# Hyena convolutions on one Trainium2 core: the spectra's complex product for both signs in single VectorE instructions

## The chip, the cores and the metric

The kernel runs on one core of one Trainium2 chip. The metric is the device time of one execution in microseconds. In three runs the kernel before took 1834.95, 1834.99 and 1835.55 us: the median is 1834.99 us.

## What is computed

Two layers of a trunk over 512 latent and 256 context tokens with 1024 features. In each layer a projection feeds three groups of heads: a bidirectional Hyena operator (256 channels), neighbourhood attention and latent attention. Their outputs are joined and projected, and a squared-ReLU MLP follows. The context is computed in layer 0 alone. The part that the change touches is the long convolution inside Hyena, twice per sequence (once per gate):

```python
def _bidir_fftconv(u, h, bias):
    L, C = u.shape[1], u.shape[2]
    k = jnp.concatenate([h[:, 0], jnp.zeros((1, C), h.dtype), h[:0:-1, 1]], axis=0)
    uf = u.astype(F32)
    y = jnp.fft.irfft(jnp.fft.rfft(uf, n=2 * L, axis=1) * jnp.fft.rfft(k, axis=0), n=2 * L, axis=1)[:, :L]
    return (y + uf * bias.astype(F32)).astype(u.dtype)

def _hyena(p, conv_w, conv_b, filt, bias):
    p = _short_conv(p, conv_w, conv_b)
    v, x1, x2 = jnp.split(p, 3, axis=-1)
    z = v
    for o, gate in enumerate((x1, x2)):
        z = gate * _bidir_fftconv(z, filt[:, o], bias[o])
    return z
```

## The kernel before

All matrix products run on TensorE in single precision; large ones are split into three products of rounded halves. VectorE, ScalarE and GpSimd do the elementwise work between, SyncE issues the loads. The program is written as Python generators, one per task; `weave` takes steps from several in turn at given rates, and a scheduler then fixes the order of the instructions on each engine before the program runs. Each engine works through its own list in that order, and waits on semaphores where a value comes from another engine.

The convolution is `hyena(l, s, y, p)`, for layer `l` and stream `s` (0: 512 latent tokens, tiles named with x; 1: 256 context tokens, tiles named with c). It is woven into the neighbourhood attention: the context's in layer 0 with the making of queries and keys (`na_qk`), the latent one of layer 0 with the attention itself (`na_attend`, lines 526 to 579), that of layer 1 with the end of `na_qk` and with `na_attend`. For each of the two orders `o` it does the following.

- The sequence is split into even and odd positions, and both are transformed by matmuls with cosine and sine tables (line 735), for one tile `ft` of 128 frequencies at a time: `ee` from the even half, `oo` from the odd half, each 128x512 in PSUM (real part and imaginary part, 256 channels each). The latent stream has n = 2 such tiles, the context n = 1.
- ScalarE copies `ee` to SBUF (`eb`, line 739). The sum `eb + oo` is the spectrum at one set of frequencies (sign 0), the difference that at the mirrored set (sign 1), line 744.
- Each is multiplied by the filter's spectrum `kk[:, ft, sgn]`, which is loaded from DRAM. A complex product takes two multiplies (lines 748 and 749, the second with real and imaginary part of the filter exchanged), a subtraction (750) and an addition (751). For sign 1 these four run on GpSimd, for sign 0 on VectorE.
- Sum and difference of the two products go to `z` (lines 753 and 754), from which TensorE transforms back: in the first order with line 763, multiplied by the gate in line 765, in the second with line 774, multiplied by the gate in line 778.

PSUM has four banks `b` here, used in turn by the transforms, by the attention's transposes (560), and by its value products (579). A bank goes to a new user when the last reader of the old one is done; the reader of `oo` is line 744. The attention's scores (526) have two larger buffers `mm`, read by the bias sum on VectorE (548) and its counterpart on ScalarE (549). The softmax then runs through VectorE's maximum (425), ScalarE's exponential (430), VectorE's reciprocal (433), and the normalization of one head on VectorE (438) and of the other on ScalarE (436).

The lines of the product before:

```python
for sgn, op in ((1, ALU.subtract), (0, ALU.add)):
    eng = pool if sgn else dve
    us = p([128, 2, 256], tag=f"us{sgn}{g}")
    dve.tensor_tensor(us, eb..., oo..., op)
    ks = kk[:, ft, sgn]
    ta = p([128, 2, 256], tag=f"ta{sgn}{g}")
    eng.tensor_tensor(ta, us, ks, ALU.mult)
    eng.tensor_tensor(us, us, ks[:, ::-1, :], ALU.mult)
```

Of the kernel before, what the change touches and what calls it, by code (L numbers as in the profile page):

```python
# [16 lines left out]
ALU = mybir.AluOpType  # L17
# [24 lines left out]
def kernel(ctx, tc, A, dbg=None, stop=None):  # L42
    nc = tc.nc
    pe, act, dve, pool, sp = nc.tensor, nc.scalar, nc.vector, nc.gpsimd, nc.sync
# [54 lines left out]
    def b_tile():  # L99
        npsum[0] += 1  # L100
        return ps.pool.tile([128, 512], F32, tag="b", name=f"b{npsum[0]}", bufs=ps.b)
# [199 lines left out]
    def load(p, name, shape, src=None, tag=None, bufs=1):  # L301
        t = p(shape, tag=tag, bufs=bufs)
        sp.dma_start(t, A[name] if src is None else src)
        return t
# [400 lines left out]
    def hyena(l, s, y, p):  # L705
        L, t0 = ((S, 0), (LC, S))[s]
        n = L // 256
        nt = 2 * n
        kd = (kx[l], kc)[s]
        g = "xc"[s]  # L710
        fc = load(p, "dft_f" + g, [128, n, 4, L // 2])
        ic = load(p, "dft_i" + g, [128, n, 4, L // 2])

        def tparity(tile_, m, tt):
            par, i = divmod(tt, n)
            v = tile_[:, m, t0:t0 + L].rearrange("p (t z) -> p t z", z=2)
            return v[:, i * 128:(i + 1) * 128, par]

        u, x1 = p([128, nt, 256], tag="u" + g, bufs=1), p([128, nt, 256], tag="x1" + g)
        for tt in range(nt):  # L720
            t = b_tile()
            for m in range(4):
                pe.transpose(t[:, m * 128:(m + 1) * 128], tparity(y, m, tt), ident)
            act.activation(u[:, tt], t[:, 0:256], AF.Copy)
            act.activation(x1[:, tt], t[:, 256:512], AF.Copy)
            yield
        for o in range(2):
            kk = load(p, None, [128, n, 2, 2, 256], kd[:, :, :, o], "kk" + g)
            z = p([128, n, 2, 2, 256], tag="z" + g)
            for ft in range(n):  # L730
                ee, oo = b_tile(), b_tile()
                for par, out in ((0, ee), (1, oo)):
                    for q in range(2):
                        for kt in range(n):
                            pe.matmul(out[:, q * 256:(q + 1) * 256],  # L735
                                      fc[:, kt, 2 * par + q, ft * 128:(ft + 1) * 128], u[:, par * n + kt],
                                      start=(kt == 0), stop=(kt == n - 1))
                eb = p([128, 512], tag="eb" + g)
                act.activation(eb, ee, AF.Copy)
                y2 = []  # L740
                for sgn, op in ((1, ALU.subtract), (0, ALU.add)):
                    eng = pool if sgn else dve
                    us = p([128, 2, 256], tag=f"us{sgn}{g}")
                    dve.tensor_tensor(us, eb.rearrange("p (i c) -> p i c", i=2),
                                      oo.rearrange("p (i c) -> p i c", i=2), op)
                    ks = kk[:, ft, sgn]
                    ta = p([128, 2, 256], tag=f"ta{sgn}{g}")
                    eng.tensor_tensor(ta, us, ks, ALU.mult)  # L748
                    eng.tensor_tensor(us, us, ks[:, ::-1, :], ALU.mult)
                    eng.tensor_sub(ta[:, 0], ta[:, 0], ta[:, 1])  # L750
                    eng.tensor_add(ta[:, 1], us[:, 0], us[:, 1])
                    y2.append(ta)
                dve.tensor_add(z[:, ft, 0], y2[1], y2[0])
                dve.tensor_sub(z[:, ft, 1], y2[1], y2[0])
                yield
            if o == 0:
                u = p([128, nt, 256], tag="u" + g, bufs=1)
                for tt in range(nt):
                    par, i = divmod(tt, n)
                    t = b_tile()  # L760
                    for ft in range(n):
                        for q in range(2):
                            pe.matmul(t[:, 0:256], ic[:, ft, 2 * par + q, i * 128:(i + 1) * 128], z[:, ft, par, q],  # L763
                                      start=(ft == 0 and q == 0), stop=(ft == n - 1 and q == 1))
                    dve.tensor_mul(u[:, tt], t[:, 0:256], x1[:, tt])
                    yield
            else:
                for ct in range(2):
                    t = b_tile()
                    h = L // 2  # L770
                    for par in range(2):
                        for ft in range(n):
                            for q in range(2):
                                pe.matmul(t[:, par * h:(par + 1) * h], z[:, ft, par, q, ct * 128:(ct + 1) * 128],  # L774
                                          ic[:, ft, 2 * par + q, :], start=(ft == 0 and q == 0),
                                          stop=(ft == n - 1 and q == 1))
                    ys = y[:, 4 + ct, t0:t0 + L].rearrange("p (t z) -> p z t", z=2)
                    dve.tensor_mul(ys, ys, t[:, :L].rearrange("p (z t) -> p z t", z=2))
                    yield
# [422 lines left out]
    for l in range(DEPTH):  # L1202
# [49 lines left out]
        if last:  # L1252
            hs = Pool(f"hy{l}", "right")
            conv = hyena(l, 0, y, hs)
        sc = Pool(f"nas{l}")
        nb = na_bias(l, bp, sc)
        if last:
            weave((na_qk(l, hh, hl, na, sc), 1.0), fill=(conv, H1))
        else:
            weave((na_qk(l, hh, hl, na, sc), 1.0), (hyena(l, 1, y, sc), 0.8))  # L1260
# [17 lines left out]
        if not last:  # L1278
            hs = Pool(f"hy{l}")
            conv = hyena(l, 0, y, hs)  # L1280
# [50 lines left out]
        for m in range(KD):  # L1331
            ks = range(8)
            if last:
                ks = range(4, 8)
# [14 lines left out]
            for s, a, b in STREAM[:len(streams)]:  # L1349
                g = gains[:, l, 1, m, s:s + 1]  # L1350
# [187 lines left out]
```

## Time and profile before

| | |
|---|---|
| median of three runs | 1834.99 us |
| profiled execution, its own time | 1833.48 us |
| span of that execution, first to last instruction | 1831.7 us |
| TensorE busy | 1752.5 us (96%) |
| VectorE busy | 1233.4 us (67%), 2247 instructions |
| ScalarE busy | 754.7 us (41%) |
| GpSimd busy | 135.8 us (7%), 177 instructions |
| mean granted TensorE clock | 0.981 of 2.4 GHz |

The profile is one execution. Its times are microseconds from the span's start; in its rows PE is TensorE, DVE VectorE, ACT ScalarE, POOL GpSimd, SP SyncE, and L748 is line 748 of the kernel. A matmul's record shows its tile, `out<-in`; single-precision matmuls of 128 rows are two records each. The context's convolution lies between 233 and 276 us, layer 0's latent one between 299 and 357 us, that of layer 1 between 1265 and 1323 us. An instruction of VectorE ends some 0.08 us after the next one has begun when neither waits for the other, so a busy time is a little longer than the distance from start to start.

### The profile page before, as it was taken

How to read it: one execution, taken by the hardware profiler on the slowest of the kernel's cores; microseconds unless marked ns; L12 is line 12 of the kernel's file. 1: busy time of each engine (PE TensorE's matmuls, PEld its weight loads, DVE VectorE, ACT ScalarE, POOL GpSimd, SP SyncE). 2: the span in 40 equal slices, each digit the busy share in tenths (PEclk: the TensorE clock that was granted, in tenths of full speed). 3: DMA queues.
4: the chain of work that ended last, by engine and by line, in shares of the span. 5: the costliest groups of instructions: out<-in, count | busy, mean ns of one | idle time of the engine just before them, and what ended most of it. 6: DMA issues, size and time to landing. Idle time of an engine off the chain costs nothing. (4 is left out here: it accounts for less than half of the span.)

```text
span 1831.7 us, 27057 instructions
## 1 busy us (share of the span) xinstructions
PE 1752.5 (96%) x10794; PEld 1499.4 (82%) x10794; DVE 1233.4 (67%) x2247; ACT 754.7 (41%) x1262; POOL 135.8 (7%) x177
## 2 busy tenths in 40 slices
PE   5999977889999999999999999999999999999999
PEld 2788976756788888888888888888777799999997
DVE  5867777787768877767665447787877665555554
ACT  3624326566734412213212224745666653333331
POOL 1134222200000000000000000231200000000000
PEclk8999989989999999999999999999999999999999
DMA  9225423263153333333332222362041022333232
GB/s 344 72 86 167 148 70 108 82 214 113 53 198 115 138 120 134 117 137 115 130 124 60 67 68 95 114 226 81 24 167 41 31 93 94 97 99 93 93 93 81
DMA packets 73389, 206.11 MB, mean 113 GB/s; under 512 B 12556, under 2 KB 24605, under 8 KB 71856
## 3 DMA queue, kind: packets, MB, share of 16 engines
q1 hardware_dynamic: 71664, 199.15, 32.3%
q0 software_dynamic: 1600, 5.24, 0.8%
q8 instruction: 85, 1.39, 0.3%
q14 instruction: 40, 0.33, 0.1%
HBM read 182.35 MB, written 21.23 MB: 111 GB/s over the span
## 5 line engine op out<-in xcount | busy, mean ns | idle before, releaser
L273 PE MATMUL mm<-t,wh 128*128 128x512 f32 (+1 forms) x2496 | 492.5, 317 | 1.9 <-DVE t L1037 1.3
L136 ACT ACTIVATE wh<-wr 128x1024 fp32r<-128x1024 f32 (+2 forms) x176 | 185.2, 1054 | 599.4 <-PE mm L273 541.4
L273 PEld LDWEIGHTS mm<-t,wh 128*128 128x128 f32 x2496 | 371.4, 189 | 37.9 <-issue 1.9
L273 PE MATMUL mm<-t,wl 128*128 128x512 f32 (+1 forms) x1248 | 296.9, 316 | 0.0
L137 DVE TENSOR_TENSOR wl<-wr,wh 128x1024 fp32r<-128x1024 f32 (+2 forms) x176 | 214.1, 1217 | 30.5 <-ACT wh L136 27.1
L273 PE MATMUL mm<-al,wh 128*128 128x512 f32 (+1 forms) x768 | 233.6, 359 | 0.0
L273 PE MATMUL mm<-ah,wl 128*128 128x512 f32 (+1 forms) x768 | 232.2, 356 | 0.0
L1037 DVE SCALAR_TENSOR_TENSOR t<-mm,mods,t 128x512 f32<-128x512 f32 x216 | 136.3, 659 | 140.6 <-PE mm L273 132.7
L273 PE MATMUL mm<-ah,wh 128*128 128x512 f32 (+1 forms) x768 | 230.9, 354 | 0.0
L273 PEld LDWEIGHTS mm<-t,wl 128*128 128x128 f32 x1248 | 193.6, 189 | 16.2 <-DVE wl L137 0.2
L273 PEld LDWEIGHTS mm<-ah,wl 128*128 128x128 f32 x768 | 127.6, 188 | 22.5
L273 PEld LDWEIGHTS mm<-ah,wh 128*128 128x128 f32 x768 | 126.7, 188 | 23.6
L273 PEld LDWEIGHTS mm<-al,wh 128*128 128x128 f32 x768 | 126.3, 188 | 20.1
L191 DVE SCALAR_TENSOR_TENSOR wmp<-wm,t 128x1024 f32<-128x1024 f32 x64 | 78.3, 1224 | 68.3 <-DMA wm<-in_w_modr_dram 68.3
L425 DVE TENSOR_REDUCE mmx<-mm 128x1 f32<-128x768 f32 (+1 forms) x80 | 67.5, 846 | 24.9 <-PE mm L133 24.2
L136 ACT ACTIVATE ah<-relu 128x768 fp32r<-128x768 f32 (+1 forms) x64 | 47.3, 739 | 87.2 <-DVE relu L1100 87.1
L430 ACT ACTIVATE msb<-mm,mmx,qrs 128x768 f32<-128x768 f32 (+1 forms) x80 | 72.2, 904 | 24.8 <-DVE mmx L427 21.1
L1090 DVE TENSOR_SCALAR bb<-mm,cols 128x2 f32<-128x2 f32 x64 | 14.0, 219 | 97.6 <-PE mm L273 97.4
L191 DVE SCALAR_TENSOR_TENSOR wm<-wm,t 128x1024 f32<-128x1024 f32 x64 | 78.1, 1220 | 0.2
L1001 ACT ACTIVATE mpt<-mm 128x768 f32<-128x768 f32 (+1 forms) x80 | 57.6, 725 | 49.9 <-PE mm L1000 49.8
L137 DVE TENSOR_TENSOR al<-relu,ah 128x768 fp32r<-128x768 f32 (+1 forms) x64 | 52.6, 823 | 36.2 <-ACT ah L136 36.1
L1346 PE MATMUL mm<-t,wh 128*128 128x512 f32 x320 | 76.2, 352 | 0.0
(304 smaller groups left out, 2922.0 us busy)
## 6 DMA issues: line engine op xcount, KB each, us to landing
wr<-in_w_ff_dram SPq DMA_DIRECT2D x128, 512.0 KB, 3.6
wm<-in_w_modr_dram SPq DMA_DIRECT2D x64, 512.0 KB, 4.5
wm<-in_w_mod_dram SPq DMA_DIRECT2D x32, 512.0 KB, 8.4
wr<-in_w_in_t_dram SPq DMA_DIRECT2D x18, 512.0 KB, 4.0
qk<-qk_spill SPq DMA_DIRECT2D x9, 576.0 KB, 5.5
qk_spill<-upk SPq DMA_DIRECT2D x12, 384.0 KB, 2.9
kx<-kk POOLq DMA_DIRECT2D x16, 256.0 KB, 2.5
wr<-in_w_in_qk_dram SPq DMA_DIRECT2D x8, 512.0 KB, 4.6
```

Source lines behind the costliest of these rows:

```text
L136: act.activation(hi, src, AF.Copy)
L137: dve.tensor_sub(lo, src, r32(hi))
L191: dve.scalar_tensor_tensor(w if s else junk, w, 1.0, cr[:, s], ALU.mult, ALU.mult, accum_out=mods[:, l, v, k, s:s + 1])
L273: pe.matmul(out_[:, po:po + b - a], wk[wx], mk[mx][:, a:b], start=(k == 0 and i == 0), stop=(k == nk - 1 and i == 2))
L425: dve.tensor_reduce(mx, src, AX.X, ALU.max, negate=True)
L430: act.activation(sb[:, h, :n], src[:, h, :n], AF.Exp, bias=mx[:, h:h + 1], scale=1.0 if scale is None else scale[:, h:h + 1], accum_out=sm ...
L1001: act.activation(pt[:, 0:nkt, qt * 128:(qt + 1) * 128], tt[:, :nkt * 128].rearrange("p (c q) -> p c q", q=128), AF.Copy)
L1037: dve.scalar_tensor_tensor(xT[:, m, a:b], t[:, a:b], mods[:, l, v, m, s:s + 1], xT[:, m, a:b], ALU.mult, ALU.add)
L1090: dve.tensor_scalar(bb, t[:, 768:770], cols[:, l, C_BF1 + f:C_BF1 + f + 1], None, ALU.add)
L1346: pe.matmul(t[:, a:b], ws[wx], half[mx][:, k % 4, a:b], start=(k == ks[0] and i == 0), stop=(k == 7 and i == 2))
```

## The change

The two signs lie side by side in one tile `us` and one tile `ta` of 2 x 2 x 256 elements a partition. The sum and the difference are still two instructions, each into its half; the two multiplies, the subtraction and the addition are one VectorE instruction each for both signs. GpSimd has no part in it. Per frequency tile VectorE's eight instructions (6 of 512 elements, two of 256) become eight (two of 1024 and six of 512), and GpSimd's four go.

```diff
-                y2 = []
-                for sgn, op in ((1, ALU.subtract), (0, ALU.add)):
-                    eng = pool if sgn else dve
-                    us = p([128, 2, 256], tag=f"us{sgn}{g}")
-                    dve.tensor_tensor(us, eb.rearrange("p (i c) -> p i c", i=2),
-                                      oo.rearrange("p (i c) -> p i c", i=2), op)
-                    ks = kk[:, ft, sgn]
-                    ta = p([128, 2, 256], tag=f"ta{sgn}{g}")
-                    eng.tensor_tensor(ta, us, ks, ALU.mult)
-                    eng.tensor_tensor(us, us, ks[:, ::-1, :], ALU.mult)
-                    eng.tensor_sub(ta[:, 0], ta[:, 0], ta[:, 1])
-                    eng.tensor_add(ta[:, 1], us[:, 0], us[:, 1])
-                    y2.append(ta)
-                dve.tensor_add(z[:, ft, 0], y2[1], y2[0])
-                dve.tensor_sub(z[:, ft, 1], y2[1], y2[0])
+
+                us, ta = p([128, 2, 2, 256], tag=f"us{g}"), p([128, 2, 2, 256], tag=f"ta{g}")
+                for sgn, op in ((0, ALU.add), (1, ALU.subtract)):
+                    dve.tensor_tensor(us[:, sgn].rearrange("p i c -> p (i c)"), eb, oo, op)
+                dve.tensor_tensor(ta, us, kk[:, ft], ALU.mult)
+                dve.tensor_tensor(us, us, kk[:, ft, :, ::-1, :], ALU.mult)
+                dve.tensor_sub(ta[:, :, 0], ta[:, :, 0], ta[:, :, 1])
+                dve.tensor_add(ta[:, :, 1], us[:, :, 0], us[:, :, 1])
+                dve.tensor_add(z[:, ft, 0], ta[:, 0], ta[:, 1])
+                dve.tensor_sub(z[:, ft, 1], ta[:, 0], ta[:, 1])
```

The new lines are 742 to 749: sums 743, multiplies 744 and 745, subtraction 746, addition 747, z 748 and 749. Everything below stands five lines higher than before (763 becomes 758, 774 becomes 769). The scheduler also orders the instructions around the product anew, in the three stretches named above and nowhere else; SyncE's list doesn't change. Three places follow.

VectorE in layer 0, context, first order. `tok` is the tile of keys that line 485 normalizes and TensorE then transposes (line 491); lines 124 to 126 are steps of a reciprocal square root, 12 columns wide. Before:

```order
L744 TENSOR_TENSOR us1c_2281<-ebc_2279,b_2274 128x512
L126 SCALAR_TENSOR_TENSOR nrs_2255<-rs_t_2256,nrs_2255 128x12
L744 TENSOR_TENSOR us0c_2288<-ebc_2279,b_2274 128x512
L124 TENSOR_TENSOR rs_t_2256<-nrs_2255 128x12
L748 TENSOR_TENSOR ta0c_2290<-us0c_2288,kkc_2270 128x512
L749 TENSOR_TENSOR us0c_2288<-us0c_2288,kkc_2270 128x512
L750 TENSOR_TENSOR ta0c_2290<-ta0c_2290 128x256
L485 TENSOR_TENSOR tok_2115<-tok_2115,nrs_2255 128x256 x3
```

Changed:

```order
L743 TENSOR_TENSOR usc_2281<-ebc_2279,b_2274 128x512
L126 SCALAR_TENSOR_TENSOR nrs_2255<-rs_t_2256,nrs_2255 128x12
L124 TENSOR_TENSOR rs_t_2256<-nrs_2255 128x12
L744 TENSOR_TENSOR tac_2282<-usc_2281,kkc_2270 128x1024
L125 SCALAR_TENSOR_TENSOR rs_t_2256<-rs_t_2256,nms_2253 128x12
L745 TENSOR_TENSOR usc_2281<-usc_2281,kkc_2270 128x1024
L746 TENSOR_TENSOR tac_2282<-tac_2282 128x2x256
L485 TENSOR_TENSOR tok_2115<-tok_2115,nrs_2255 128x256 x3
```

The same steps stand ahead of line 485 in the same places (a few small ones and the second sum are left out here); only their widths differ.

VectorE in layer 1, latent, first order, from the end of the first tile into the second. `nsb` is the attention's softmax tile. Before:

```order
L753 TENSOR_TENSOR zx_11607<-ta0x_11629,ta1x_11622 128x512
L754 TENSOR_TENSOR zx_11607<-ta0x_11629,ta1x_11622 128x512
L425 TENSOR_REDUCE nmx_11654<-nsb_11637 128x2
L744 TENSOR_TENSOR us1x_11675<-ebx_11673,b_11664 128x512
L744 TENSOR_TENSOR us0x_11682<-ebx_11673,b_11664 128x512
L548 SCALAR_TENSOR_TENSOR nsb_11692<-mm_11691,t_10293,t_11080 128x256
L748 TENSOR_TENSOR ta0x_11684<-us0x_11682,kkx_11605 128x512
L433 RECIPROCAL nrc_11659<-nsm_11656 128x2
L438 TENSOR_SCALAR nsb_11637<-nsb_11637,nrc_11659 128x512
L749 TENSOR_TENSOR us0x_11682<-us0x_11682,kkx_11605 128x512
```

Changed:

```order
L425 TENSOR_REDUCE nmx_11612<-nsb_11595 128x2
L748 TENSOR_TENSOR zx_11571<-tax_11585 128x512
L749 TENSOR_TENSOR zx_11571<-tax_11585 128x512
L743 TENSOR_TENSOR usx_11633<-ebx_11631,b_11622 128x512
L433 RECIPROCAL nrc_11617<-nsm_11614 128x2
L438 TENSOR_SCALAR nsb_11595<-nsb_11595,nrc_11617 128x512
L744 TENSOR_TENSOR tax_11634<-usx_11633,kkx_11569 128x1024
L548 SCALAR_TENSOR_TENSOR nsb_11644<-mm_11643,t_10257,t_11044 128x256
L745 TENSOR_TENSOR usx_11633<-usx_11633,kkx_11569 128x1024
```

The maximum of the softmax (425) went from behind z to ahead of it, the normalization (438) from behind the first multiply to ahead of it.

TensorE in layer 0, latent, second order, where z of the second tile is used for the first time. Before:

```order
L560 MATMUL b_3356<-ident,nsb_3204 128x128 x2
L560 MATMUL b_3361<-ident,nsb_3204 128x128 x2
L774 MATMUL b_3317<-t_2739,zx_3174 128x256 x6
L774 MATMUL b_3366<-t_2739,zx_3174 128x256 x8
L526 MATMUL mm_3376<-t_1293,t_1291 128x256 x2
L526 MATMUL mm_3376<-t_1294,t_1291 128x256 x2
L526 MATMUL mm_3376<-t_1293,t_1292 128x256 x2
L579 MATMUL b_3394<-npt_3308,t_90 64x128
```

Changed:

```order
L526 MATMUL mm_3340<-t_1293,t_1291 128x256 x2
L526 MATMUL mm_3340<-t_1294,t_1291 128x256 x2
L769 MATMUL b_3330<-t_2727,zx_3150 128x256 x2
L526 MATMUL mm_3340<-t_1293,t_1292 128x256 x2
L579 MATMUL b_3358<-npt_3272,t_90 64x128
L579 MATMUL b_3358<-npt_3279,t_90 64x128
L769 MATMUL b_3281<-t_2727,zx_3150 128x256 x6
L769 MATMUL b_3330<-t_2727,zx_3150 128x256 x6
```

The scores of the next attention unit and a whole value product (eight rows of 579, two of them shown) went from behind the products with z to ahead of them.

## Rows read from the trace of the kernel before

**Rows 1.** Timeline of TensorE, context: start, length, engine, line, operation, [idle before <-releaser].
```profile
244.35 1.05 PE L491 MATMUL b<-ident,tok 128*128 128x128 f32 x3 [4.18 <-DVE tok L485]
...
268.29 1.20 PE L774 MATMUL b<-t,zc 128*128 128x128 f32 x4 [4.06 <-DVE zc L753]
```

**Rows 2.** Timeline of TensorE, layer 0, latent.
```profile
314.31 2.09 PE L763 MATMUL b<-zx,t 128*128 128x256 f32 x8 [1.49 <-issue]
...
319.99 0.33 PE L560 MATMUL b<-ident,nsb 128*128 128x128 f32 x1 [1.77 <-DVE t L137]
...
344.65 1.10 PE L774 MATMUL b<-t,zx 128*128 128x256 f32 x4 [0.87 <-DVE us0x L744]
...
350.81 6.31 PE L774 MATMUL b<-t,zx 128*128 128x256 f32 x28 [2.88 <-DVE zx L753]
```

**Rows 3.** Timeline of TensorE, layer 1, latent.
```profile
1275.91 1.06 PE L560 MATMUL b<-ident,nsb 128*128 128x128 f32 x8 [1.19 <-DVE nsb L438]
...
1282.94 1.06 PE L560 MATMUL b<-ident,nsb 128*128 128x128 f32 x8 [2.88 <-DVE nsb L438]
...
1310.83 1.13 PE L774 MATMUL b<-t,zx 128*128 128x256 f32 x4 [3.13 <-DVE us0x L744]
```

**Rows 4.** Windows: stretch, length, TensorE busy (records), granted clock, DMA share, GB/s.
```profile
240.00:252.00 12.00, 6.99 (x34) 0.72 0.12 44
264.00:276.00 12.00, 7.94 (x47) 0.72 0.00 0
318.00:328.00 10.00, 7.96 (x48) 0.83 0.31 107
1282.00:1290.00 8.00, 7.06 (x35) 0.79 0.37 131
1308.00:1318.00 10.00, 6.51 (x42) 0.83 0.00 0
```

**Rows 5.** Timeline of VectorE, layer 0, latent, first order.
```profile
301.00 0.49 DVE L438 TENSOR_SCALAR nsb<-nsb,nrc 128x512 f32<-128x512 f32 x1
...
303.76 0.68 DVE L744 TENSOR_TENSOR us1x<-ebx,b 128x512 f32<-128x512 f32 x1
304.36 0.68 DVE L744 TENSOR_TENSOR us0x<-ebx,b 128x512 f32<-128x512 f32 x1
...
305.52 0.83 DVE L748 TENSOR_TENSOR ta0x<-us0x,kkx 128x512 f32<-128x512 f32 x1
306.27 1.49 DVE L438 TENSOR_SCALAR nsb<-nsb,nrc 128x512 f32<-128x512 f32 x1
...
319.85 0.68 DVE L753 TENSOR_TENSOR zx<-ta0x,ta1x 128x512 f32<-128x512 f32 x1
```

**Rows 6.** Timeline of GpSimd in the same stretch.
```profile
304.52 1.27 POOL L748 TENSOR_TENSOR ta1x<-us1x,kkx 128x512 f32<-128x512 f32 x1 [37.59 <-DVE us1x L744]
305.87 1.60 POOL L749 TENSOR_TENSOR us1x<-us1x,kkx 128x512 f32<-128x512 f32 x1
```

**Rows 7.** Groups by form (count, busy, mean ns), then line 749 (ns min/median/max).
```profile
L137 DVE TENSOR_TENSOR wl<-wr,wh 128x1024 fp32r<-128x1024 f32 x170 | 208.4, 1226 | 28.8 <-ACT wh L136 25.4
...
L749 DVE TENSOR_TENSOR us0c<-us0c,kkc x2: 679/1160/1642, 241.7 to 263.9; 128x512 f32<-128x512 f32 x2
```

**Rows 8.** Timeline of VectorE, context, first and second order.
```profile
237.96 0.68 DVE L744 TENSOR_TENSOR us1c<-ebc,b 128x512 f32<-128x512 f32 x1
...
243.26 1.61 DVE L485 TENSOR_TENSOR tok<-tok,nrs 128x256 f32<-128x256 f32 x3
...
261.15 0.69 DVE L744 TENSOR_TENSOR us1c<-ebc,b 128x512 f32<-128x512 f32 x1 [0.49 <-PE b L735]
...
267.47 0.68 DVE L753 TENSOR_TENSOR zc<-ta0c,ta1c 128x512 f32<-128x512 f32 x1
```

**Rows 9.** Timeline of VectorE, layer 0, latent, second order.
```profile
335.32 0.68 DVE L744 TENSOR_TENSOR us1x<-ebx,b 128x512 f32<-128x512 f32 x1
...
350.08 0.68 DVE L753 TENSOR_TENSOR zx<-ta0x,ta1x 128x512 f32<-128x512 f32 x1
```

## The prediction

> **What bounds the kernel now.** I read the page's busy shares first (TensorE 96%), then TensorE's timeline around the convolutions for the places where it does stand still, then the granted clock there, then VectorE and GpSimd in the same microseconds. TensorE rarely waits in this kernel, but the Hyena convolutions are one of the places, and what it waits for is VectorE. In the context's convolution it stands 4.18 us for the normalized keys (line 485, queued on VectorE between the steps of the product) and 4.06 us for the product z itself [rows 1]. In layer 0's latent convolution the waits are 1.49 (a PSUM bank that the next tile's second sum still reads), 1.77 (a copy queued behind the product), 0.87 (a bank again) and 2.88 (z) [rows 2]; in layer 1's 1.19 and 2.88 (the softmax's normalization, line 438, queued on VectorE) and 3.13 (a bank that a sum releases) [rows 3]. Around each cluster the granted clock drops from 2.4 to 1.2 GHz: 12 us at a mean of 0.72 are 2 x 0.28 x 12 = 6.7 us at the lower level, twice; 10 us at 0.83 and 8 us at 0.79 are 3.4 us each, three times [rows 4]. A microsecond of matmul at the lower level costs half a microsecond, so up to 3.4 us hang on each of the first two and 1.7 on each of the other three.
>
> VectorE is busy there, and part of that is waiting that counts as busy. The multiply of line 748 starts at 305.52 and ends at 306.35, 0.56 after GpSimd's own multiply ended (304.52 + 1.27 = 305.79); the normalization of line 438 that follows takes 1.49 where it takes 0.49 alone, and ends 0.29 after GpSimd's second multiply [rows 5, 6]. Sums with one input in PSUM keep their 0.68 while GpSimd works. So VectorE and GpSimd take turns where both read SBUF, and the "parallel" half of the product holds up the other half, and the softmax with it.
>
> **The change part by part.** There are ten frequency tiles: one per order for the context, two per order for each layer's latent tokens.
>
> *Removed:* 40 GpSimd instructions, near 5 us per tile. Nothing else ran on GpSimd there; with them goes the wait of z for GpSimd.
>
> *Added on VectorE, per tile:* two sums 512 wide (as before), two multiplies 1024 wide, two combinations of 2x256, two sums into z. A 512-wide one costs 0.60 from start to start (303.76 to 304.36) [rows 5]. No 1024-wide product stands in the trace; the nearest row is the subtraction of two 1024-wide SBUF operands, 1.226 [rows 7], so 1.15 start to start. The reversed operand order costs nothing by itself: the same form 512 wide took 679 ns at its fastest, GpSimd idle [rows 7]. Bounds for the multiply: 1.15 below, and two of the slowest held-up ones above, 2 x 1.64 = 3.3 [rows 7]; I take 1.15, since the delay has GpSimd as its cause and GpSimd is gone. A tile's own work is then 6 x 0.60 + 2 x 1.15 = 5.9 us.
>
> *Context, first order.* Line 485 started 5.30 us after the first sum and its three took 1.61 [rows 8]. Now 2 x 0.60 + 2 x 1.15 + 0.60 and four tiny steps (0.1 each, my estimate) stand ahead, 4.5, and the three cost 3 x 0.34: the last ends 1.4 earlier. Next late is z, behind one combination and a small reduction; TensorE gains 1.2.
>
> *Context, second order.* First sum to z took 6.32 [rows 8]; now 1.2 + 2.3 + 1.2 and the same 0.8 of other work between, 5.5: 0.8 gained.
>
> *Layer 0 latent, first order.* First sum to the second tile's z took 319.85 - 303.76 = 16.1 [rows 5]. Now 2 x 5.9 less the last two sums, 10.6, and between them four bias sums (half as wide, 0.40 each, my estimate), two normalizations 0.82, two reciprocals 0.3, a copy 0.2 and two softmax maxima (1024 wide, 2.3; only one of them stood ahead of z before): 15.8. Walking TensorE through its new rows: the 1.49 becomes 0.65 (the bank comes free 0.45 earlier, with score matmuls moved ahead of it), the 1.77 becomes 1.4 (a score bank instead of the copy), and 0.9 for z in place of 0.3: 0.6 gained.
>
> *Layer 0 latent, second order.* First sum to second z took 350.08 - 335.32 = 14.8 [rows 9]; now 10.6 and 3.1 of other work, 13.7. The 0.87 falls to 0.1, since the tiles' sums end 0.8 earlier. In the 2.88 TensorE's order now has scores and a value product, 0.6 + 1.0, that stood behind: 2.88 - 1.1 - 1.6 is 0.2. Together 3.5 gained: the largest term, and half of it is order.
>
> *Layer 1, first order.* Both normalizations move ahead of multiplies. Between the first tile's z and the next normalization stood a maximum, two sums, two bias sums, a held-up multiply (0.8 or more) and a reciprocal, 4.1; now two sums and a reciprocal, 1.3. So 1.19 and 2.88 go, or nearly. But the maximum (1.15) now stands ahead of z, which comes 0.5 later on the first tile and 1.2 earlier on the second, and the walk finds waits of 1.2, 1.1 and 1.0 in their place: 0.8 gained.
>
> *Layer 1, second order.* The bank of the 3.13 us wait comes 0.5 earlier and 0.3 of score matmuls move ahead of it: 0.7 gained, and about as much left for z as before.
>
> *What is late next* everywhere is z again or the softmax. No DMA moves; SyncE's queue is the same row for row. Waits sum to 1.2 + 0.8 + 0.6 + 3.5 + 0.8 + 0.7 = 7.6 us.
>
> *The clock.* The three short drops follow waits that become shorter or are broken up, so each may go: 1.7 each. The two long ones follow waits that remain near 3 us; they probably stay. Everything behind moves by some microseconds, so later drops may come or go too. I count one short drop as gone: 7.6 + 1.7 = 9.3. The profiled execution took 1833.48 us (span 1831.7), so 1824.2 for it; the median of the runs is 1.5 higher, 1834.99, so **1825.7**.
>
> A rule speaks against merging. The row first: the normalization that TensorE waits 2.88 us for [rows 3] is a short instruction queued behind wide ones. The Trainium skill (Perfetto Trace Analysis, "Optimizing Scalar/DVE Operations") says that where VectorE isn't saturated but causes bubbles elsewhere, breaking instructions up may let work finish sooner. By it the sum would lose what the latent convolutions gain on VectorE; that is the third rival.
>
> **The rivals.** A change measured at under 0.2%, 3.7 us, can't be told from none.
> - *Shorter waits, but every drop stays or a new one comes.* For it: the remaining waits of about 1 us stand close together. 7.6 less up to 1.7: 1827.4 to 1829. Chance 0.2.
> - *All short drops go and the long ones shorten.* 7.6 + 5.1, and perhaps 2 more: 1820 to 1822. For it: the three follow waits that are at least partly removed. Against: the bank wait in layer 1 keeps some 2.3 us. Chance 0.18.
> - *Head of the line.* Wide multiplies and the maximum ahead of z delay short work as much as the lock did, so that the latent terms lose their VectorE part, 0.6 + 1.9 + 0.8 + 0.7 of the 7.6, and z is later by 0.5 in four orders: 3.6 - 2 = 1.6 left, 1833.4. For it: two of my walks give a later first z. Against: VectorE's total falls. Chance 0.16, all of it no change.
> - *The merged multiplies don't run at 1.15.* If the pattern of four dimensions with a reversed one costs 2.3, twenty multiplies cost 23 us more, of which at least half lies ahead of z: 11.5 - 7.6 + 0.5 for a further drop, 1839.4, slower. It decides from 0.4 us more per multiply, 1.55 (7.6 / 20). Against: the reversed form at 679 ns [rows 7]. Chance 0.06.
>
> **How the numbers follow.** The forecast has 0.4. Faster: 0.4 + 0.2 + 0.18 = 0.78; same 0.16; slower 0.06. The range leaves out the slower case, the far end of "all drops go" and a little of the head-of-line case: 1819.0 to 1834.5. The likeliest case alone is 1823 to 1828.
>
> **What would show it.** Right: line 438 back to 0.5 us in these stretches, the 1024-wide multiplies at 1.2, GpSimd's busy time down by some 50 us of its 136, VectorE's no higher than 1233; the 2.88 us before the last product of layer 0 gone; the waits for 438 in layer 1 gone, with waits for z or a score bank in their place. Wrong: multiplies over 1.55, or TensorE's idle time in the six places within 3 us of before, or the gain in them given back later, for instance by a lower clock at the start of the latent attention.

## The result and the profile after

The changed kernel took **1821.06 us** (median of four runs, 1819.58 to 1826.58) against 1835.27 for the kernel before in the same runs: ratio 0.9922, 95% interval 0.9902 to 0.9942. Timed again on another chip it took 1820.41 against 1835.90, ratio 0.9914 (0.9897 to 0.9932). So it is 14 to 15.5 us faster. The forecast was 9.3 us, with 1819.0 to 1834.5 as its range; the time came out where the rival "all short drops go and the long ones shorten" had put it, 1820 to 1822.

The page's busy times of the changed kernel, of its first profile (this execution took 1826.58, the longest of the four):

```profile
PE 1750.7 (96%) x10794; PEld 1498.3 (82%) x10794; DVE 1226.0 (67%) x2247; ACT 754.5 (41%) x1262; POOL 89.6 (5%) x137
```

GpSimd lost 46.2 us, VectorE 7.4, though it now does the whole product. On VectorE's groups by form (context and layer 0; count, busy, mean ns) the instructions have the lengths of an undisturbed engine, also line 438, which took 1.49 us in [rows 5]:

```profile
L744 DVE TENSOR_TENSOR tax<-usx,kkx 128x1024 f32<-128x1024 f32 x4 | 4.9, 1220 | 0.0
L745 DVE TENSOR_TENSOR usx<-usx,kkx 128x1024 f32<-128x1024 f32 x4 | 4.9, 1218 | 0.0
L438 DVE TENSOR_SCALAR nsb<-nsb,nrc 128x512 f32<-128x512 f32 x8 | 3.9, 483 | 0.1
```

TensorE's timeline at the places of [rows 1] (first two lines), [rows 2] (next two) and [rows 3] (the last three); line numbers behind the product are five lower after the change:

```profile
245.72 1.05 PE L491 MATMUL b<-ident,tok 128*128 128x128 f32 x3 [2.93 <-DVE tok L485]
...
269.34 1.20 PE L769 MATMUL b<-t,zc 128*128 128x128 f32 x4 [3.47 <-DVE zc L748]
...
319.13 1.99 PE L758 MATMUL b<-zx,t 128*128 128x256 f32 x8 [0.87 <-DVE zx L748]
...
345.93 5.45 PE L769 MATMUL b<-t,zx 128*128 128x256 f32 x24
...
1276.54 1.97 PE L758 MATMUL b<-zx,t 128*128 128x256 f32 x8 [1.04 <-issue]
...
1284.90 2.86 PE L758 MATMUL b<-zx,t 128*128 128x256 f32 x12 [0.87 <-DVE zx L748]
...
1312.55 5.45 PE L769 MATMUL b<-t,zx 128*128 128x256 f32 x24 [0.75 <-DVE zx L748]
```

The waits of 2.88 before the last product of layer 0 and for line 438 in layer 1 are gone. What is left in the latent convolutions is 1.58 us in one place (a score bank in layer 0) and 1.04 or less in all others. The context keeps its two waits, 2.93 and 3.47.

To add this up I cut each profile at landmarks that both kernels have: VectorE's first sum of the context, its first sum of the latent convolution, and the first matmul of the latent attention (line 960, now 955) behind it. This gives three stretches: the context's convolution, layer 0's latent one, layer 1's. First the kernel before, then the changed one, by windows; the fourth line of each is what lies between layer 0's attention and layer 1's convolution.

```profile
237.96:303.76 65.80, 50.94 (x350) 46.61 (x349) 43.29 (x102) 27.37 (x66) 9.85 (x8) 0.84 0.31 96
303.76:363.47 59.71, 51.89 (x401) 41.36 (x398) 48.29 (x91) 34.04 (x90) 18.83 (x16) 0.97 0.13 49
1269.76:1329.30 59.54, 51.47 (x385) 41.44 (x381) 50.41 (x87) 35.45 (x83) 19.20 (x16) 0.94 0.06 22
363.47:1269.76 906.29, 886.68 (x5264) 756.35 (x5266) 631.40 (x1160) 353.33 (x563) 25.17 (x44) 0.99 0.36 123
```
```profile
240.68:302.73 62.05, 49.14 (x350) 44.64 (x348) 41.17 (x102) 27.23 (x66) 0.00 (x0) 0.89 0.33 102
302.73:355.45 52.72, 50.19 (x397) 40.21 (x396) 45.21 (x91) 34.52 (x90) 0.00 (x0) 1.00 0.17 62
1268.63:1322.74 54.11, 48.92 (x384) 39.50 (x380) 47.42 (x87) 35.56 (x83) 0.00 (x0) 1.00 0.07 24
355.45:1268.63 913.18, 888.92 (x5264) 760.14 (x5266) 632.06 (x1161) 353.08 (x563) 26.95 (x44) 0.98 0.36 122
```

The columns after the length are busy time (and records) of TensorE, its weight loads, VectorE, ScalarE and GpSimd, then granted clock, DMA share and GB/s. The three stretches took 185.05 us and take 168.88: 16.17 less. Length less TensorE's busy time is its idle time, 30.75 before and 20.63 after: 10.1 us of the gain. The other 6.05 are TensorE's busy time for nearly the same matmuls (1131 records against 1136): the clock, which is now at its upper level through both latent stretches. The stretches of [rows 4] in the changed kernel (the fourth 2 us earlier):

```profile
240.00:252.00 12.00, 7.97 (x43) 6.93 (x42) 9.17 (x22) 1.15 (x3) 0.00 (x0) 0.72 0.13 44
264.00:276.00 12.00, 8.53 (x61) 8.33 (x61) 8.35 (x23) 2.17 (x6) 0.00 (x0) 0.86 0.00 0
318.00:328.00 10.00, 9.11 (x64) 7.41 (x61) 8.54 (x20) 8.09 (x20) 0.00 (x0) 1.00 0.23 83
1280.00:1288.00 8.00, 6.23 (x48) 5.05 (x49) 7.85 (x16) 4.67 (x12) 0.00 (x0) 1.00 0.37 131
1308.00:1318.00 10.00, 8.27 (x50) 6.74 (x51) 8.92 (x18) 6.56 (x16) 0.00 (x0) 1.00 0.01 2
```

All three short drops are gone. Of the two long ones the first stayed, 0.72 over 12 us as before, and the second is half as long, 0.86. The context's stretch has a third long drop that [rows 4] doesn't show: in the kernel before it lies at 291 to 299 us, behind waits of 3.73 us for a score bank and 2.02 us for line 438, with 6.8 us at the lower level. In the changed kernel the second of these waits is 1.10, and 3.4 us stand at the lower level. By windows of 1 us, 30.7 us of the three stretches ran at the lower level before and 13.6 do now.

In this one execution 6.9 us of the gain were lost again between the convolutions (fourth lines), and 2.7 ahead of the context's first sum. Of the 6.9 us, 2.2 are busy time of TensorE, at a clock of 0.98 against 0.99, and 4.7 idle time, half of it in one wait for ScalarE's tile `hu` (line 615), 6.1 us against 3.8. The instructions on TensorE are the same ones in the same order there, and the second profile of the changed kernel has neither loss: 906.08 us in the middle, 238.17 to the first sum, 168.69 in the three stretches. So these losses vary between executions and are no price of the change.

### The profile page after: what moved, and what is told of

The parts are those of the page before. It is cut to its first block, busy times and chain, and to the rows that moved or that the text cites. A ratio compares the mean times of both kernels' runs of the same rounds, so it can differ in the third digit from the quotient of the medians.

```text
span 1824.7 us, 26988 instructions
## 1 busy us (share of the span) xinstructions
PE 1750.7 (96%) x10794; PEld 1498.3 (82%) x10794; DVE 1226.0 (67%) x2247; ACT 754.5 (41%) x1262; POOL 89.6 (5%) x137
## 4 chain that ended last, share of the span: by engine, by line
PE 86%; DVE 6%; ACT 4%; DMA 2%; issue 2%; POOL 0%; SPq 0%; DVEq 0%; ACTq 0%; POOLq 0%
PE mm L273 54%; PE mm L1341 5%; PE b L1008 3%; PE mm L995 3%; PE mm L131 2%; PE mm L133 2%; PE mm L132 2%; PE b L387 2%; PE b L131 1%; PE b L150 1%; PE b L132 1%; PE b L133 1%; PE b L350 1%; PE b L1049 1%; PE b L758 1%
## 5 line engine op out<-in xcount | busy, mean ns | idle before, releaser
L137 DVE TENSOR_TENSOR wl<-wr,wh 128x1024 fp32r<-128x1024 f32 (+2 forms) x176 | 213.9, 1216 | 30.7 <-ACT wh L136 27.4
L273 PEld LDWEIGHTS mm<-ah,wh 128*128 128x128 f32 x768 | 126.9, 188 | 23.4
```

The costliest lines, as they stand in the source:

```text
L137: dve.tensor_sub(lo, src, r32(hi))
L273: pe.matmul(out_[:, po:po + b - a], wk[wx], mk[mx][:, a:b], start=(k == 0 and i == 0), stop=(k == nk - 1 and i == 2))
```

## The experiments

My theory, A, was that VectorE and GpSimd hold each other up where both read SBUF (the lock, for short), and that this is what TensorE waited for. The rivals: B, that fewer and wider instructions are what helps; C, that the scheduler, given other instructions, put VectorE's and TensorE's work in a better order.

**1. No GpSimd, nothing merged.** In the kernel before:

```diff
-                    eng = pool if sgn else dve
+                    eng = dve
```

> The kernel before with both signs' products on VectorE in the old 512-wide steps: nothing on GpSimd, nothing merged. If taking GpSimd's reads of SBUF away is what matters (theory A), nearly all of the gain is here: a tile costs 6.2 us of VectorE instead of 5.9, line 438 takes 0.5 us everywhere, and the time is 1820 to 1825. If the merging (fewer, wider instructions) is what matters (theory B), VectorE gets 46 more instructions and the time is 1829 to 1836. If it is the scheduler's new order of TensorE's work (theory C), the time lies in between, by how much of that order this kernel shares: 1826 to 1831, with the 2.88 us before the last product of layer 0 mostly back.

Measured: 1834.57 us against 1833.73, ratio 0.9996 (0.9979 to 1.0013). A alone has fallen: the lock is gone (line 438, 512 wide, takes 0.48 us everywhere), GpSimd's busy time is down by 48 us, VectorE is busy for 1226.4 us (1226.0 in the changed kernel), and the median shows no gain. The time lies in the range for B and above that for C, and C's sign did not come either: the 2.88 us before the last product of layer 0 are not back. Yet this run doesn't show B, since the scheduler made a third order for this kernel: compared by the traces, over 150 of TensorE's 10794 matmuls stand in another place than in the kernel before, and over 150 in another than in the changed kernel. In layer 1, TensorE and VectorE read:

```profile
1277.43 1.06 PE L560 MATMUL b<-ident,nsb 128*128 128x128 f32 x8 [2.85 <-DVE nsb L438]
```
```profile
1270.92 0.68 DVE L753 TENSOR_TENSOR zx<-ta0x,ta1x 128x512 f32<-128x512 f32 x1
1271.53 0.68 DVE L754 TENSOR_TENSOR zx<-ta0x,ta1x 128x512 f32<-128x512 f32 x1
...
1273.14 1.22 DVE L425 TENSOR_REDUCE nmx<-nsb 128x2 f32<-128x1024 f32 x1
...
1276.22 0.67 DVE L748 TENSOR_TENSOR ta0x<-us0x,kkx 128x512 f32<-128x512 f32 x1
1276.81 0.47 DVE L438 TENSOR_SCALAR nsb<-nsb,nrc 128x512 f32<-128x512 f32 x1
```

This is the wait of 2.88 of [rows 3], without any GpSimd. The softmax's maximum (line 425) stands behind the sums into z and a sum of the next tile, starts 8.60 us after the first sum (1264.54), and line 438 follows 12.27 us after it. In the changed kernel's trace the same instructions stand the other way round:

```profile
1272.61 0.48 DVE L438 TENSOR_SCALAR nsb<-nsb,nrc 128x512 f32<-128x512 f32 x1
...
1274.62 1.22 DVE L425 TENSOR_REDUCE nmx<-nsb 128x2 f32<-128x1024 f32 x1
1275.76 0.68 DVE L748 TENSOR_TENSOR zx<-tax 128x512 f32<-128x512 f32 x1
...
1278.22 0.48 DVE L438 TENSOR_SCALAR nsb<-nsb,nrc 128x512 f32<-128x512 f32 x1
1278.61 1.22 DVE L744 TENSOR_TENSOR tax<-usx,kkx 128x1024 f32<-128x1024 f32 x1
```

The maximum starts 5.99 us after the first sum (1268.63) and line 438 9.59 us after it, ahead of the multiply: 2.7 us earlier. So in layer 1 this wait was one of order.

**2. The lock put back, order kept.** In the changed kernel, after the copy of the even half:

```diff
+                d, fv = p([128, 512], tag="d" + g), fc[:, ft].rearrange("p a t -> p (a t)")[:, 0:512]
+                pool.tensor_copy(d[:, 0:1], eb[:, 0:1])
+                for _ in range(5):
+                    pool.tensor_tensor(d, fv, fv, ALU.mult)
```

> The changed kernel, and beside each tile's product GpSimd makes five 512-wide products of a table in SBUF that nobody uses; on all other engines the instructions stand in the same order as in the changed kernel, and no one waits for GpSimd's results. Theory A (VectorE and GpSimd hold each other up where both read SBUF): line 438 and the product's instructions are long again (up to 1.5 us for 0.5, 1.7 and more for 1.2) wherever GpSimd works, and 8 to 14 us of the gain are lost: 1829 to 1836. If GpSimd was only the slow half of the product for which z waited, or if the new order is the cause (C), the time stays within 2 us of the changed kernel, 1819 to 1823.

Measured: 1850.47 us, ratio 1.0080 (1.0056 to 1.0105), 16.7 slower than the kernel before and 30 slower than experiment 3 on the same chip. Nobody waits for GpSimd's results here, and the other engines' order is the changed kernel's, row for row; the same three groups as above, and the sum that has an input in PSUM, read:

```profile
L749 DVE TENSOR_TENSOR usx<-usx,kkx 128x1024 f32<-128x1024 f32 x4 | 6.5, 1632 | 0.0
L748 DVE TENSOR_TENSOR tax<-usx,kkx 128x1024 f32<-128x1024 f32 x4 | 6.0, 1506 | 0.0
L747 DVE TENSOR_TENSOR usx<-ebx,b 128x512 f32<-128x512 f32 x8 | 5.2, 676 | 1.3 <-PE b L735 1.3
L438 DVE TENSOR_SCALAR nsb<-nsb,nrc 128x512 f32<-128x512 f32 x8 | 4.6, 578 | 0.1
```

The lock is real: multiplies of 1.22 us take 1.51 and 1.63, the sum keeps its 0.68. The loss is beyond my 8 to 14, with 69 us more of GpSimd work, where the change had taken 46 away.

**3. The same with writes only.**

```diff
-                for _ in range(5):
-                    pool.tensor_tensor(d, fv, fv, ALU.mult)
+                for _ in range(8):
+                    pool.memset(d, 0.0)
```

> The same, with eight 512-wide memsets on GpSimd instead of the products: GpSimd is busy beside the product and writes SBUF, but reads none. Theory A as I state it (both read SBUF): VectorE's durations stay as in the changed kernel, and the time is within 2 us of it, 1819 to 1823. If any GpSimd work in SBUF holds VectorE up, line 438 is over 0.7 us in these stretches and the time is 1825 or more.

Measured: 1820.76 us, ratio 0.9919 (0.9895 to 0.9942), the changed kernel's time.

```profile
L748 DVE TENSOR_TENSOR tax<-usx,kkx 128x1024 f32<-128x1024 f32 x4 | 4.9, 1214 | 0.0
L438 DVE TENSOR_SCALAR nsb<-nsb,nrc 128x512 f32<-128x512 f32 x8 | 3.9, 482 | 0.1
```

44 us more of GpSimd work that only writes SBUF (but for a copy one column wide in each tile) stretch nothing. The Trainium skill (SBUF — State Buffer, "Who interferes with whom") states the same: a VectorE instruction with two SBUF inputs contends with a GpSimd one that reads SBUF, not with one that only writes it. The traces of these two runs agree: the multiply took 1214 ns beside the memsets, 1506 and 1632 ns beside the products.

**4. Only the context's two tiles merged**, the new code for the context, the old one for the latent tokens:

```diff
+                if s:
...
+                    dve.tensor_tensor(ta, us, kk[:, ft], ALU.mult)
...
+                else:
...
+                        eng = pool if sgn else dve
```

> Only the context's two tiles merged, the latent tiles as before with GpSimd; TensorE's and ScalarE's order is that of the kernel before. Waits of 1.2 and 0.8 us go, and by the two traces the two stretches of the context's convolution shorten by 1.1 and 2.7 us, part of it clock. Theory A: 1831 to 1833.5. If the gain there is an accident of these two traces (clock drops that come and go with anything), no difference: 1834 to 1836, or a gain over 5 us from drops elsewhere.

Measured: 1834.89 us, ratio 1.0000 (0.9987 to 1.0014): no gain. That is outside my range for A and inside the one for "an accident of these two traces". Its profile does have the context's stretch at 61.99 us, 3.8 less than before, but the latent one of layer 0, whose code is the old one, took 61.15, 1.4 more (clock 0.92), and what lies between that and layer 1's convolution 910.9, 4.6 more. The local gain is there, and does not reach the end; one profile doesn't show whether the later losses come from the edit or vary by themselves.

**5 and 6. The changed kernel and experiment 1 once more, side by side.**

> The changed kernel once more, on the chip of the three next ones. Its six convolution stretches (from the context's first sum to the last product of each layer) are 160 us together against 173 before; if that is the whole gain, it is 1819 to 1823 again and the ratio 0.990 to 0.995. If the gain of the first timing was partly luck with the clock elsewhere, 1824 to 1828.

> The kernel of the first experiment again, for a second profile: its first one, 1828.0, was the fastest of its twelve runs and showed 164 us in the convolution stretches, 9 less than before, while the median showed no gain. If what it lacks is lost outside the convolutions by the clock's chance (theory C1), this profile has 163 to 166 us there and 4 to 8 us more at the lower clock elsewhere, and the median is again 1832 to 1836. If the convolution stretches themselves vary from run to run (C2), they are 168 to 174 us here.

Measured: 1820.41 (ratio 0.9914, 0.9897 to 0.9932) and 1832.72 (0.9982, 0.9968 to 0.9996). So without GpSimd and without merging, in the order that the scheduler made for that kernel, the gain is 0 to 3 us, and 12 to 14 us stand between that kernel and the changed one. By the cut of these two expectations (from the context's first sum to the last product of each layer) the convolutions took 159.9 us in the changed kernel and 168.9 in the other. The two profiles of experiment 1's kernel, layer 0's latent stretch:

```profile
301.86:358.12 56.26, 51.04 (x398) 40.52 (x397) 46.82 (x109) 35.31 (x90) 0.00 (x0) 1.00 0.15 56
```
```profile
302.28:361.67 59.39, 54.16 (x404) 42.59 (x400) 46.97 (x109) 35.38 (x90) 0.00 (x0) 0.94 0.14 53
```

The same program, the same idle time (5.22 and 5.23), and 3.13 us between them, all clock. So C2 held and C1 fell: the stretches themselves vary, because a drop comes in one execution and not in another.

**7. Only the multiplies split by sign**, in the changed kernel (the second multiply likewise):

```diff
-                dve.tensor_tensor(ta, us, kk[:, ft], ALU.mult)
+                for sgn in range(2):
+                    dve.tensor_tensor(ta[:, sgn], us[:, sgn], kk[:, ft, sgn], ALU.mult)
```

> The changed kernel with only its two 1024-wide multiplies split by sign into four 512-wide ones; combinations stay merged, nothing on GpSimd. VectorE's busy time rises by 20 x 0.05 = 1 us. If the width of the multiplies matters by itself, the time is that of the kernel of the first experiment, 1831 to 1836. If only the order that the scheduler makes matters (theory C), it lies anywhere between 1819 and 1836, and the stretch of layer 1's first order shows why: either line 438 waits behind a product (a wait near 2.9 us, 32 to 33 us for the stretch) or it doesn't (29 us).

Measured: 1826.45 us, ratio 0.9947 (0.9930 to 0.9963), 6 slower than the changed kernel on the same chip. Layer 1's first order takes 30.09 us, between the 29 and the 32 to 33 that I had named, and there two waits for line 438 are back (total us, times, longest):

```profile
PE b L560 <- DVE nsb L438: 1.9, 2, 1.6
```

**8. The product first.** In the changed kernel, and nothing else:

```diff
+                with tc.high_priority(60):
...
+                    dve.tensor_tensor(ta, us, kk[:, ft], ALU.mult)
...
```

> The changed kernel's instructions in another order: the steps of the product get a higher priority in the scheduler, so that the sums into z stand ahead of the softmax's maxima. If order is worth as much as the removed lock (theory C), the time moves by 4 us or more: to 1812 to 1817 where z was the late one, or to 1825 to 1834 where the softmax is late instead. If the order matters little (theory A alone), 1819 to 1823.

Measured: 1831.72 us, ratio 0.9975 (0.9962 to 0.9988): 11 us of the gain gone by order alone, the instructions being the same. TensorE's waits in layer 1:

```profile
PE mm L526 <- ACT nsb L549: 5.3, 2, 4.3
PE b L770 <- ACT npt L562: 1.7, 2, 1.2
```

It waits for the softmax, 4.3 us in one piece for a bank of scores.

**9. The lock in the dose of the kernel before**, experiment 2 with

```diff
-                for _ in range(5):
-                    pool.tensor_tensor(d, fv, fv, ALU.mult)
+                for w in (512, 512, 256, 256):
+                    pool.tensor_tensor(d[:, 0:w], fv[:, 0:w], fv[:, 0:w], ALU.mult)
```

> The changed kernel with the dose of GpSimd work that the kernel before had, two products 512 wide and two 256 wide per tile, again of a table that nobody uses; all other engines' order is that of the changed kernel. Five 512-wide ones cost 30 us, with 69 us more of GpSimd. If the loss goes by GpSimd's busy time, 46 us of it cost 20: 1838 to 1843, more than the kernel before, which had its own order and GpSimd did useful work there. If it is waits that only the long GpSimd blocks cause, 1822 to 1830.

Measured: 1838.69 us against 1836.07, ratio 1.0021 (1.0007 to 1.0035); by the ratios 1.0 to 1.1%, some 19 us, over the changed kernel. It isn't quite "the old work in the new order", since VectorE does the whole product as well. VectorE's busy time grows by only 11 us over the changed kernel's; TensorE's idle time in the three stretches goes from 20.6 to 30.9, and the clock falls with it:

```profile
239.76:304.67 64.91, 49.15 (x338) 44.70 (x336) 42.69 (x103) 27.35 (x66) 6.62 (x9) 0.84 0.32 98
304.67:365.79 61.12, 54.85 (x398) 43.19 (x397) 49.91 (x92) 34.43 (x90) 18.69 (x20) 0.92 0.15 53
1273.47:1334.20 60.73, 51.86 (x385) 41.66 (x381) 52.20 (x87) 35.67 (x83) 17.66 (x18) 0.94 0.06 22
```

**10 and 11. The softmax further ahead**, experiment 8 with

```diff
-                with tc.high_priority(60):
+                with tc.high_priority(-20):
```

and with -60.

> The changed kernel's instructions with the product's steps at a lower priority (by 20), so that in the latent convolutions the softmax's steps stand further ahead of them. The product first gave 1831.7. If the softmax is what TensorE waits for in layer 1, as line 438 was, this gains 2 to 5 us: 1815 to 1819. If the changed kernel's order is already past the best point, z is late instead and it is 1823 to 1830.

> The same by 60, which also moves the keys' normalization (line 485) ahead of the product in the context's convolution, where TensorE waits 3.0 us for it and 3.5 for z. If the two waits only trade places, the two context stretches stay at 22.0 and 39.9 us; if line 485 was the worse one, they lose 1 us or more. In all 1814 to 1820 if softmax first is better, 1824 to 1832 if z is late instead.

Measured: 1832.23 (ratio 0.9976, 0.9963 to 0.9989) and 1831.30 (0.9973, 0.9960 to 0.9985). Both lose, experiment 10 more than the 1823 to 1830 that I had put there. They go too far to the other side: now z is what comes late. Of experiment 10, layer 1:

```profile
PE b L759 <- DVE zx L749: 3.0, 1, 3.0
PE b L770 <- DVE zx L749: 2.9, 1, 2.9
```

In experiment 11's context TensorE still waits 3.0 us for line 485 and 3.7 before the last product, and the two orders take 22.2 and 42.7 us (22.1 and 39.9 in the changed kernel): nothing is won there.

**12. Split multiplies, order mended.** Experiment 7 with its steps at a lower priority:

```diff
+                with tc.high_priority(-8):
...
+                    for sgn in range(2):
+                        dve.tensor_tensor(ta[:, sgn], us[:, sgn], kk[:, ft, sgn], ALU.mult)
...
```

> The seventh experiment's kernel (the two wide multiplies split by sign) with its steps at a lower priority by 8, which brings TensorE's and ScalarE's order back to nearly that of the changed kernel: 21 and 22 rows differ from it, where 83 and 130 did. If the order made the seventh experiment lose 6 us (theory C), this one is within 2 us of the changed kernel: 1819 to 1822.5, and layer 1's first order takes 29.0 to 29.5 us. If splitting itself costs it (20 more instructions, and others that fall between the halves), it stays at 1824 to 1829.

Measured: 1824.03 us, ratio 0.9933 (0.9920 to 0.9946). That misses the range for C and lies at the lower end of the other. Layer 1's first order takes 29.09 us (30.09 in experiment 7, 29.01 in the changed kernel), as I had expected under C. Its idle time in the three stretches is 21.1 us, near the changed kernel's 20.6; its profile has the context at a clock of 0.81. So of the 6 us that splitting cost, the mended order brought back 2.4, and the intervals of the two ratios overlap. What is left, 2 to 3.6 us, this run can't assign: it may be width by itself (B), or order, which isn't quite the same; the latent stretches are 1.0 us longer each. The two combinations of 2x256 were never split in the changed kernel's order, so what their merging is worth by itself isn't shown.

All of them together, by the three stretches of one profile each (length, TensorE's idle time in them) and the timing:

| kernel | length | idle | median us | ratio to before |
|---|---|---|---|---|
| before | 185.05 | 30.75 | 1835.27 | 1 |
| changed (first, again) | 168.88, 168.69 | 20.6, 20.9 | 1821.06, 1820.41 | 0.9922, 0.9914 |
| 3 memsets on GpSimd | 169.18 | 21.0 | 1820.76 | 0.9919 |
| 12 split, order mended | 173.25 | 21.1 | 1824.03 | 0.9933 |
| 7 multiplies split | 173.98 | 24.3 | 1826.45 | 0.9947 |
| 8 product first | 179.55 | 27.1 | 1831.72 | 0.9975 |
| 10 softmax first | 180.55 | 23.4 | 1832.23 | 0.9976 |
| 11 softmax first, more | 182.70 | 27.7 | 1831.30 | 0.9973 |
| 1, 6 no GpSimd, unmerged | 178.75, 183.65 | 28.0, 27.3 | 1834.57, 1832.72 | 0.9996, 0.9982 |
| 4 context only | 182.31 | 27.5 | 1834.89 | 1.0000 |
| 9 GpSimd, four products | 186.76 | 30.9 | 1838.69 | 1.0021 |
| 2 GpSimd, five products | 199.86 | 42.2 | 1850.47 | 1.0080 |

The first column sorts the kernels nearly as the timing does, though each length is that of one execution: the profile of experiment 10 is its longest of twelve, the first of experiment 1 its shortest. Experiment 10 has little idle time and is slow nevertheless: its waits are few and long, and the granted clock in its three stretches is 0.89, 0.97 and 0.89.

## Why the prediction came out as it did

**The time was inside the range, 4.6 us under the forecast; most waits were walked well, and the clock was under-counted.** Term by term, idle time first:

- *Context, 1.2 + 0.8.* Idle time fell from 14.86 to 12.91, 1.95: right. The wait for line 485 went from 4.18 to 2.93, that for z from 4.06 to 3.47, both still near 3, as said.
- *Layer 0 latent, 0.6 + 3.5.* It fell from 7.82 to 2.53, 5.3. The largest term was right, the 0.87 and the 2.88 being gone altogether. In the first order the bank wait that I left at 0.65 is gone too; the score bank and z took 1.58 and 0.87, where I had 1.4 and 0.9.
- *Layer 1, 0.8 + 0.7.* It fell from 8.07 to 5.19, 2.9. The first order's waits for z and a score bank came (1.04, 0.25, 0.74, 0.87, against my 1.2, 1.1, 1.0). The failed size is in the second order: "the bank wait in layer 1 keeps some 2.3 us" did not happen. Before, TensorE's first product with z stood until the second tile's last sum gave a bank free (3.13 us). In the changed kernel's trace that product starts at 1304.59, ahead of the end of these sums (1306.24), and only 0.47 behind z; 0.75 for z and 0.79 for a copy follow.
- *The clock, 1.7.* This is the step that failed: "I count one short drop as gone". All three went, and TensorE's busy time fell by 1.70 in layer 0 and 2.55 in layer 1. Of the long ones, which "probably stay", the first did and the second halved; the third, at 291 us, which the forecast doesn't have, halved as well: 1.80 in the context. Together 6.05 against 1.7. The rival that came nearest, "all short drops go and the long ones shorten", had a chance of 0.18, and the argument against it rested on the 2.3 us of the bank wait.

7.6 + 1.7 = 9.3 was the sum; 10.1 + 6.05 = 16.2 is what the stretches show, and 14.2 and 15.5 what the timings do.

**The reason was half right.** "The 'parallel' half of the product holds up the other half, and the softmax with it": the lock is there, as I read it from [rows 5, 6], and it is dear (19 us in the changed kernel's order, 30 with half as much GpSimd work again). But taking it away, in the order that the scheduler made for that kernel, gained 0 to 3 us (experiments 1 and 6). The changed kernel's order with the lock is as slow as the kernel before or slower (experiment 9); the changed kernel's instructions, with the product earlier or later, keep about a third of the gain (8, 10, 11). Neither part does it alone. I had counted order as half of one term; with the lock gone, 11 us of the gain hung on it. It was in my walks all the same: that both normalizations move ahead of multiplies and that maxima now stand ahead of z was read from the order, and priced. Not shown is how much of experiment 1's loss against the changed kernel is order and how much its narrower instructions: no run has them in the changed kernel's order, and experiment 12, the nearest, leaves up to 3.6 us open for the multiplies.

- *Head of the line* ended as no gain in my rivals. Its mechanism exists, and experiment 10 shows it at full size (z late by 3.0 and 2.9 us in layer 1); the changed kernel's order lies short of the point where it decides.
- *The rule on breaking instructions up* (the Trainium skill, Perfetto Trace Analysis, "Optimizing Scalar/DVE Operations") spoke against the merge. Here splitting the multiplies cost 6 us, and 2 to 3.6 with the order mended: no run shows a gain from it.
- *The multiplies* ran at 1.22 us, 1.13 to 1.15 from start to start, against 1.15; that rival is out.

## What to carry to other kernels

Where an engine's work is ordered by a scheduler, an edit of a few instructions is two edits: what they cost, and where everything else lands. Test the two apart: put the old cost back beside the new order, and move the order with the instructions kept. And where TensorE waits for one engine that serves two customers in turn (here z and the softmax), here time was won by dividing the waits between the two, not by serving either first.

GpSimd work "beside" VectorE is no free parallelism where both read SBUF: 11 us of stretched VectorE instructions cost 19 us of the kernel here, since TensorE waited behind them (10.3 us more idle time in the three stretches) and its clock fell (7.6 us more busy time).

## What was not expected

- **The same program drops its clock in one execution and not in another.** Experiment 1's kernel ran layer 0's latent stretch at a clock of 1.00 once and 0.94 once, with idle times 0.01 us apart; the middle of the changed kernel took 913.18 us once and 906.08 once, 4.3 of the difference being busy time and 2.8 idle time. What settles it stays open. A stage's gain read from one profile can be 3 us off for this reason alone. The spread of one program's times varies as well: twelve runs of experiment 1's kernel went from 1828.0 to 1841.9 us, twelve more, as experiment 6, from 1830.5 to 1835.3.
- **A local gain may not arrive.** Experiment 4 took 3.8 us out of the context's stretch and gained nothing measurable.
- No order that I tried was better than the one that the scheduler made for the merged instructions; none of the kernels is faster than the changed one, and only experiment 3, which has its order, is level with it.
